# A bidirectional encoder trunk on one core: short convolution's projections leave PSUM by ScalarE, a cross product becomes one operation, and the filling products come in another order

## The chip, the cores and the metric

The kernel runs on one core of one Trainium2 chip. The metric is the device time of one launch in microseconds (us). PE is the matrix engine (TensorE), DVE is VectorE, ACT is ScalarE, POOL is GpSimd, and SP is the engine whose queue issues most of the DMA transfers. Each engine takes its own instructions strictly in order.

## The reference, cut to what matters

One layer over 1024 tokens of width 1024, all in float32. A normalised input `h` is multiplied by one wide matrix. Its columns feed four token mixers and 32 gates; the mixers' outputs are gated and added, and cross attention and a feed-forward network follow. The change touches the mixers named S5, RG-LRU and short convolution.

```
hr, hi = a2r*b1r - a2i*b1i + b2r, a2r*b1i + a2i*b1r + b2i          # S5: complex h_t = a h_{t-1} + b_t
r  = sigmoid(xc @ wa + ba);  i = sigmoid(xc @ wx + bx)             # RG-LRU, per direction, xc = conv4(xr)
la = -8 * r * softplus(-lam)
h  = scan(exp(la), sqrt(-expm1(2 * la)) * (i * xc))                # h_t = exp(la)_t h_{t-1} + b_t
y  = b_gate * conv3(c_gate * xin)                                  # short convolution
decay = exp(gam_c - gam_d) for c >= d                              # gated DeltaNet, in the phase behind
```

## The kernel before, in words

Channels lie on the 128 partitions and the 1024 tokens along the free axis. A projection of 128 output columns is 48 matmuls of 128x512 (three products of split float32 halves, `mm3`), called from L171. PE's order is written by hand: two matmuls are one *step*, so a projection is 24 steps. Projections that nothing else orders stand in a queue of generators (`Fill`), and `fill(n)` pulls n steps from it between the matmuls of the S5 mixer. So while DVE works through S5's sequential recurrence, PE works off the queue.

The queue holds six gates (a gate is one projection and a tanh on ACT, `tho`, stored to DRAM as `thd`) and four *pairs*. `pair(j)` interleaves `lru(j)` with `short_conv(j)`. PE's order in a pair is: LX 24 steps, LG 24, la0 2, SC 24, li0 2, SX 24, la1 2, SB 24, li1 2. LX, LG, SC, SX and SB are projections. la0, li0, la1 and li1 are small products with `lw` (L403 before, L407 after). Between them ACT and DVE compute the two directions of the RG-LRU, in the tiles `la`, `li`, `lt`, `hf`, `gl`, and the short convolution, in `sa` and `sb`.

Projections and small products share the PSUM pool `pp`, which has **two** tiles of 128x1024. PE can't start a product until the one two before it has been read out of PSUM. The order of the other engines is fixed when the kernel is built; each weight block of 128x512 is also split into two halves there, `wh` by ACT and `wl` by POOL.

The stretch of the program around the change runs in this order: `s5_in` (eight parts, 52 steps of fill), `Scalars.run` (70 steps; it needs the small weights `wba` and a table `cst`, loaded into boxes of S-phase's ring), `s5_scan` (17 turns of 16 steps), 12 steps, `s5_out` (eight parts of 12), 48 steps, `s5_glu` (four parts of 6, which read S5's output back from DRAM: `zbuf`, `cm`, `H`), then the rest of the queue, 82 steps. Then comes the DeltaNet phase (`GPhase`). Its tiles take the room of the S phase, so its first loads (`w<-in_cst`) wait for the last store of that phase (`yd<-hf`). They feed casts on DVE (`gcr`), products on POOL (`Bn`, `G`, `dgl`), and these the first matmuls of `decays` (L990 and L992 before, L993 and L995 after), ahead of which PE has one projection, Q/K/V block 4.

All tiles in the ring have one buffer per name. Line numbers in the kernel after the change are 3 to 5 higher.

Of the kernel before, what the change touches and what calls it, by code (L numbers as in the profile page):

```python
# [11 lines left out]
F32 = mybir.dt.float32  # L12
F32R = mybir.dt.float32r
AF = mybir.ActivationFunctionType
# [4 lines left out]
P = 128  # L19
# [5 lines left out]
ADD, SUB, MUL, MAX, MIN = ALU.add, ALU.subtract, ALU.mult, ALU.max, ALU.min  # L25
# [292 lines left out]
class SPhase:  # L318
# [25 lines left out]
    def short_conv(self, j):  # L344
        K, nc = self.K, self.nc
        pc = yield from self.project(SC + j)
        c = self.big("sa")
        nc.scalar.activation(c, pc, AF.Copy)
        yield False
        px = yield from self.project(SX + j)  # L350
        K.tt(c, px, c, MUL)
        cv = self.big("sb")
        K.conv(cv, c, K.v("sconv", 3 * j, 3), 1)
        yield False
        pb = yield from self.project(SB + j)
        K.tt(cv, pb, cv, MUL)
        nc.sync.dma_start(K.yd[3, j], cv)
        yield False

# [25 lines left out]
    def lru(self, j):  # L385
        K, nc = self.K, self.nc
        lw = self.ring.tile([P, 2, 2, P], F32, name="lw")
        nc.sync.dma_start(lw, K.a["lw"][j])
        xc = self.big("xc")
        K.conv(xc, (yield from self.project(LX + j)), K.v("lconv", 4 * j, 4), 2, K.v("lconvb", j))  # L390
        yield False
        pg = yield from self.project(LG + j)
        gl = self.big("gl")
        nc.scalar.activation(gl, pg, AF.Gelu_apprx_tanh)
        yield False
        hs = []
        for d in range(2):
            i = 4 * d + j
            tg = []
            for k, b in ((0, self.hba), (1, self.hbx)):  # L400
                ps = K.pp.tile([P, S], F32, name="pp")
                for o in (0, 512):
                    nc.tensor.matmul(ps[:, o:o + 512], lw[:, k, d], xc[:, o:o + 512], start=True, stop=True)  # L403
                    if o == 0:
                        yield True
                t = self.big(("la", "li")[k])
                nc.scalar.activation(t, ps, AF.Tanh, bias=b[:, i:i + 1], scale=0.5)  # L407
                tg.append(t)
                yield False
            thr, thi = tg  # L410
            a, t2 = thr, self.big("lt")
            nc.scalar.activation(t2, thr, AF.Tanh, bias=self.c4[:, i:i + 1], scale=self.c4[:, i:i + 1])
            nc.scalar.activation(a, thr, AF.Exp, bias=self.c2n[:, i:i + 1], scale=self.c2n[:, i:i + 1])
            K.stt(a, a, 1.0, t2, ADD, MUL)
            K.ts(a, a, -1.0, 1.0, MUL, ADD)
            nc.scalar.activation(t2, t2, AF.Sqrt)
            K.stt(t2, a, 1.0, t2, ADD, MUL)
            K.stt(thi, thi, 1.0, xc, ADD, MUL)
            K.tt(thi, thi, t2, MUL)
            h = self.big("hf") if d == 0 else t2  # L420
            r = (lambda x: x) if d == 0 else (lambda x: x[:, ::-1])
            nc.vector.tensor_tensor_scan(r(h), r(a), r(thi), 0.0, MUL, ADD)
            hs.append(h)
        K.tt(hs[0], hs[0], hs[1], ADD)
        K.stt(hs[0], hs[0], 0.5, gl, MUL, MUL)
        nc.sync.dma_start(K.yd[2, j], hs[0])
# [127 lines left out]
    def s5_in(self):  # L554

        K, nc, fill = self.K, self.nc, self.fill
        s5 = self.s5
        late = []
        for o in range(8):
            t = self.tmps()  # L560
            self.cmul(self.apb, s5[:, 0], s5[:, 1], o, t)
            wb = [self.ring.tile([P, 4, 8, 16], F32, name=f"wb{d}") for d in range(2)]
            lo, hi = slice(0, 64), slice(64, P)
            for i, op in ((0, SUB), (1, ADD)):
                K.tt(t[2 * i], t[2 * i], t[2 * i + 1], op)
                r = (lo, hi)[i]
                nc.scalar.activation(wb[0][r], t[2 * i][lo], AF.Copy)
                nc.vector.tensor_copy(wb[1][r], t[2 * i][hi])
            u = self.load_u(o)
            wt = []  # L570
            for i in range(2):
                ps = K.sm.tile([P, 4, P], F32, name="sm")
                for g in range(4):
                    nc.tensor.transpose(ps[:, g], t[2 * i][:, g], K.ident)
                wt.append(self.ring.tile([P, 4, P], F32, name=f"wt{i}"))
                nc.scalar.activation(wt[i], ps, AF.Copy)
            L = self.big("L").rearrange("p (g n) -> p g n", g=4)[0:16, :, 0:240]
            for q in range(2):
                pl = K.sm.tile([P, 512], F32, name="sm")[0:16, 0:480].rearrange("p (g n) -> p g n", g=2)
                for g2 in range(2):  # L580
                    g = 2 * q + g2
                    c0 = 64 * o + 16 * g
                    cf, cb = [x[:, c0:c0 + 16] for x in self.cd]
                    nc.tensor.matmul(pl[:, g2, 0:P], cf, wb[0][:, g], start=True, stop=False)
                    nc.tensor.matmul(pl[:, g2, P - 16:P], cb, wb[1][:, g, 0], start=False, stop=True)
                    nc.tensor.matmul(pl[:, g2, P:240], cb, wb[1][:, g, 1:8], start=True, stop=True)
                nc.scalar.activation(L[:, 2 * q:2 * q + 2], pl, AF.Copy)
            tT = self.ring.tile([P, 4, P], F32, name="tT", bufs=2)
            for k in range(8):
                nc.sync.dma_start(tT[16 * k:16 * k + 16], L[:, :, (7 - k) * 16:(7 - k) * 16 + P])  # L590
            for i in range(2):
                pv = K.sm.tile([P, 4, P], F32, name="sm")
                for g in range(4):
                    nc.tensor.matmul(pv[:, g], wt[i][:, g], u[:, g], start=True, stop=True)
                c0 = 32 * i + 4 * o
                h = self.H[:, :, c0:c0 + 4].rearrange("p c g -> p g c")
                nc.scalar.activation(h[0:64], pv[0:64], AF.Copy)
                nc.vector.tensor_copy(h[64:P, :, ::-1], pv[64:P])
            late.append((o, tT))
            fill(5)  # L600
            if o:
                self.s5_turn(*late.pop(0))
        fill(12)
        self.s5_turn(*late.pop(0))
# [19 lines left out]
    def s5_scan(self):  # L624

        K = self.K
        H = self.H.rearrange("p (a k) n -> p a k n", k=8)
        t0, t1 = [self.big(f"cm{i}").rearrange("p (a n) -> p a n", a=16) for i in range(2)]

        def turn(out, a, x):  # L630
            n = x.shape[1]
            ri = lambda y: y.rearrange("p n (r g) -> p n r g", r=2)
            b = lambda y: y.unsqueeze(1).to_broadcast([P, n, 64])
            for r in range(2):
                y = slice(32 * r, 32 * r + 32), slice(32 - 32 * r, 64 - 32 * r)
                K.tt(t1[:, :n, y[0]], b(a[1])[:, :, y[0]], x[:, :, y[1]], MUL)
            K.tt(out[:, :n], b(a[0]), x, MUL)
            K.tt(out[:, :n], out[:, :n], t1[:, :n], ADD)

        for k in range(1, 8):  # L640
            turn(t0, self.a8, H[:, :, k - 1])
            K.tt(H[:, :, k], H[:, :, k], t0, ADD)
            yield
        for a in range(1, 16):
            turn(t0, self.a64, H[:, a - 1:a, 7])
            K.tt(H[:, a:a + 1, 7], H[:, a:a + 1, 7], t0[:, 0:1], ADD)
            if a % 5 == 0:
                yield
        for k in range(7):
            turn(t0, self.a8, t0[:, 0:15] if k else H[:, 0:15, 7])  # L650
            K.tt(H[:, 1:16, k], H[:, 1:16, k], t0[:, 0:15], ADD)
            yield
# [1241 lines left out]
def tile_trunk(ctx, tc, a, out):  # L1894
    ctx.enter_context(tc.manual_schedule(engines={mybir.EngineType.PE}))
    K = _K(ctx, tc, a)
    nc = tc.nc
    big = ctx.enter_context(tc.tile_pool(name="big", bufs=1))
    h = big.tile([P, 2, KD, S], F32R, name="big")
    hh, hl = h[:, 0], h[:, 1]  # L1900
# [13 lines left out]
    fill = Fill()  # L1914
    with tc.tile_pool(name="tho", bufs=1, side="right") as tp, ExitStack() as gs:
        gates = [gate_tile(K, tp, i, hh, hl) for i in range(32)]
        sc = Scalars(K, gs)
        with ExitStack() as c:
            s = SPhase(K, c, hh, hl, fill)
            fill.add(*gates[:5])  # L1920
            for j in range(4):
                fill.add(s.pair(j))
            fill.add(*gates[5:6])
            s.s5_prep()
            s.s5_c()
            s.lru_prep()
# [2 lines left out]
            s.s5_in()  # L1929
            waits = [12, 12, 46, 0]  # L1930
            scan = s.s5_scan()
            for go in sc.run(hh, hl, s.parts("xc", "gl", "cm0")):
                if not go:
                    fill(waits.pop(0))
            K.lo = "pool"
# [11 lines left out]
        with ExitStack() as c:  # L1947
            g = GPhase(K, c, hh, hl, fill, sc)
# [49 lines left out]
```

## Time and profile before

| | |
|---|---|
| time, median of 3 runs | 2467.16 us (2465.7 to 2467.51) |
| time of the profiled execution | 2468.41 us |
| span of the profiled execution | 2466.6 us |
| mean granted clock of PE | 0.981 |

The span is what the trace covers; the time of the same execution is 1.8 us longer, and it is 1.25 us above the median. The granted clock is the share of its full 2.4 GHz that PE was given; 0.50 is its lower level, 1.2 GHz.

### The profile page before, as it was taken

Reading aid. Unit: us, or ns where it says so; the run is one execution under the profiler, and the core shown is the slowest. Engines: PE = TensorE matmul, PEld = TensorE weight load, DVE = VectorE, ACT = ScalarE, POOL = GpSimd, SP = SyncE. Lnnn points to the kernel's source line nnn. Section 1 sums busy time; section 2 is a strip of 40 time slices with the busy share of each in tenths; the row PEclk is TensorE's granted clock in tenths of the full one; section 3 lists DMA queues with packets and bytes.
Section 4 is the critical chain, followed back from the end, with each engine's and each line's share of the span. In section 5 each row is a group of like instructions: output and inputs, shape, how many; then the busy total and the mean of one; then the engine's idle time right before and its main releaser. Section 6 shows DMA issues by size and latency. Waiting matters only on the chain. (4 is left out here: it accounts for less than half of the span.)

```text
span 2466.6 us, 31800 instructions
## 1 busy us (share of the span) xinstructions
PE 2367.3 (96%) x11495; PEld 1924.4 (78%) x11495; DVE 1501.5 (61%) x2991; ACT 932.7 (38%) x1461; POOL 886.9 (36%) x636
## 2 busy tenths in 40 slices
PE   7999989899999999999999999999999999999998
PEld 6777767778878788787778888888788888877886
DVE  5883998845937758569336543274777666661421
ACT  6372434534324123232222133255444444443431
POOL 6422224435324233232122222204344444445443
PEclk8999999999999999999999999999999999999998
DMA  7443112432211211111165443106322222245541
GB/s 261 115 109 101 36 63 77 116 133 75 69 45 50 65 49 55 60 56 65 48 238 176 149 152 123 45 1 200 99 77 78 85 95 77 86 146 180 186 163 55
DMA packets 136205, 250.44 MB, mean 102 GB/s; under 512 B 15344, under 2 KB 42992, under 8 KB 135920
## 3 DMA queue, kind: packets, MB, share of 16 engines
q1 hardware_dynamic: 136048, 248.41, 31.3%
q8 instruction: 91, 1.49, 0.3%
q14 instruction: 66, 0.54, 0.1%
HBM read 188.58 MB, written 57.67 MB: 100 GB/s over the span
## 5 line engine op out<-in xcount | busy, mean ns | idle before, releaser
L142 POOL TENSOR_TENSOR wl<-wr,wh 128x512 fp32r<-128x512 f32 x507 | 694.0, 1376 | 1333.6 <-ACT wh L140 1146.2
L171 PE MATMUL pp<-big,wh 128*128 128x512 f32 x2560 | 728.7, 402 | 16.2 <-DVE sa L192 12.5
L140 ACT ACTIVATE wh<-wr 128x512 fp32r<-128x512 f32 (+1 forms) x526 | 322.2, 621 | 983.9 <-PE pp L171 517.7
L171 PEld LDWEIGHTS pp<-big,wh 128*128 128x128 f32 x2560 | 474.3, 191 | 118.5 <-DVE sa L192 14.8
L171 PE MATMUL pp<-big,wl 128*128 128x512 f32 x1280 | 406.4, 399 | 0.0
L1479 PE MATMUL sm<-big,wh 128*128 128x512 f32 x1152 | 363.1, 396 | 4.6 <-DVE big L142 2.5
L1479 PE MATMUL sm<-bigq,wh 128*128 128x512 f32 x1040 | 327.2, 396 | 4.2 <-ACT sm L1691 3.0
L171 PEld LDWEIGHTS pp<-big,wl 128*128 128x128 f32 x1280 | 237.7, 190 | 48.1
L1479 PEld LDWEIGHTS sm<-big,wh 128*128 128x128 f32 x1152 | 217.7, 189 | 55.9 <-DVE big L142 3.8
L1479 PEld LDWEIGHTS sm<-bigq,wh 128*128 128x128 f32 x1040 | 195.9, 189 | 51.7 <-ACT sm L1691 3.4
L1479 PE MATMUL sm<-big,wl 128*128 128x512 f32 x576 | 226.3, 393 | 0.0
L1479 PE MATMUL sm<-bigq,wl 128*128 128x512 f32 x520 | 203.9, 392 | 0.0
L171 PE MATMUL pp<-yhl,wh 128*128 128x512 f32 x512 | 137.3, 390 | 2.4 <-DVE acc L189 1.3
L1479 PEld LDWEIGHTS sm<-big,wl 128*128 128x128 f32 x576 | 109.1, 189 | 24.5
L1479 PEld LDWEIGHTS sm<-bigq,wl 128*128 128x128 f32 x520 | 98.0, 188 | 22.0
L171 PEld LDWEIGHTS pp<-yhl,wh 128*128 128x128 f32 x512 | 95.9, 188 | 23.5 <-DVE acc L189 1.7
L189 DVE SCALAR_TENSOR_TENSOR pp<-ut,vec,pp 128x1023 f32<-128x1023 f32 x88 | 113.0, 1284 | 1.6
L192 DVE TENSOR_TENSOR bigq<-bigq,sm 128x512 f32<-128x512 f32 x16 | 10.9, 684 | 125.1 <-PE sm L1479 125.1
L1758 ACT ACTIVATE pp<-ut,vec 128x1024 f32<-128x1024 f32 x44 | 53.2, 1210 | 69.2 <-DVE ut L192 69.2
L192 DVE TENSOR_TENSOR y<-y,t 128x8 f32<-128x8 f32 (+30 forms) x248 | 79.3, 359 | 0.0
L171 PE MATMUL pp<-yhl,wl 128*128 128x512 f32 x256 | 78.8, 389 | 0.0
L192 DVE TENSOR_TENSOR t<-rb,x 128x8 f32<-128x8 f32 (+30 forms) x248 | 78.4, 355 | 0.0
(417 smaller groups left out, 3337.8 us busy)
## 6 DMA issues: line engine op xcount, KB each, us to landing
wr<-in_wi SPq DMA_DIRECT2D x144, 256.0 KB, 2.7
wr<-in_wup SPq DMA_DIRECT2D x88, 256.0 KB, 4.2
wr<-in_wdn SPq DMA_DIRECT2D x80, 256.0 KB, 4.2
thd<-tho SPq DMA_DIRECT2D x32, 512.0 KB, 2.9
thi<-thd SPq DMA_DIRECT2D x32, 512.0 KB, 4.1
gd<-sg SPq DMA_DIRECT2D x22, 512.0 KB, 2.9
gr<-gd SPq DMA_DIRECT2D x44, 256.0 KB, 4.1
wr<-in_wkv SPq DMA_DIRECT2D x32, 256.0 KB, 3.7
```

Of the source, the lines that this page charges most:

```text
L140: self.nc.scalar.activation(hi, src, AF.Copy)
L142: e.tensor_tensor(lo, src, hi.bitcast(F32), SUB)
L171: self.nc.tensor.matmul(ps[:, o:o + step], w[:, i], r[:, k, o:o + step], start=first, stop=last)
L189: self.nc.vector.scalar_tensor_tensor(out, in0, s, in1, op0, op1)
L192: (eng or self.nc.vector).tensor_tensor(out, a, b, op)
L1479: self.K.nc.tensor.matmul(ps, a[:, i], b, start=start and i == 0 and j == 0, stop=last and stop is not False, skip_group_check=stop is Non ...
L1758: K.nc.scalar.activation(c[b], t[b], AF.Identity, bias=K.v("fconvb", n), scale=K.v("fconv", 3 * n + 1))
```

## The change

Five edits. Short convolution's SX and SB products are copied out of PSUM by ACT into a new box `sc`, and DVE multiplies from there; `s5_in` takes the same box for its `wb`. In the RG-LRU the step `1 - a` goes from a DVE operation to an ACT one. In the S5 recurrence two products on halves of 32 columns become one product on a view with the halves swapped. The queue's order becomes gates 0 to 2, pair 0, gates 3 to 5, pairs 1 to 3 (before: gates 0 to 4, pairs 0 to 3, gate 5). And `Scalars.run` takes other boxes.

```
         px = yield from self.project(SX + j)
-        K.tt(c, px, c, MUL)
+        x = self.big("sc")
+        nc.scalar.activation(x, px, AF.Copy)
+        K.tt(c, x, c, MUL)
         cv = self.big("sb")
         K.conv(cv, c, K.v("sconv", 3 * j, 3), 1)
         yield False
         pb = yield from self.project(SB + j)
-        K.tt(cv, pb, cv, MUL)
+        x = self.big("sc")
+        nc.scalar.activation(x, pb, AF.Copy)
+        K.tt(cv, x, cv, MUL)
...
             K.stt(a, a, 1.0, t2, ADD, MUL)
-            K.ts(a, a, -1.0, 1.0, MUL, ADD)
+            nc.scalar.activation(a, a, AF.Identity, bias=1.0, scale=-1.0)
             nc.scalar.activation(t2, t2, AF.Sqrt)
...
-            wb = [self.ring.tile([P, 4, 8, 16], F32, name=f"wb{d}") for d in range(2)]
+            wb = self.big("sc").rearrange("p (d g t j) -> p d g t j", d=2, g=4, t=8)
+            wb = [wb[:, d] for d in range(2)]
...
-            for r in range(2):
-                y = slice(32 * r, 32 * r + 32), slice(32 - 32 * r, 64 - 32 * r)
-                K.tt(t1[:, :n, y[0]], b(a[1])[:, :, y[0]], x[:, :, y[1]], MUL)
+            K.tt(ri(t1[:, :n]), ri(b(a[1])), ri(x)[:, :, ::-1], MUL)
...
-            fill.add(*gates[:5])
-            for j in range(4):
+            fill.add(*gates[:3], s.pair(0), *gates[3:6])
+            for j in range(1, 4):
                 fill.add(s.pair(j))
-            fill.add(*gates[5:6])
...
-            for go in sc.run(hh, hl, s.parts("xc", "gl", "cm0")):
+            for go in sc.run(hh, hl, s.parts("L", "cm1", "cm0")):
```

ACT's order at the second direction (la1) of pair 0, before. `sb<-sa` starts short convolution's second convolution, `lt<-lt` is the square root:

```order
L203 ACTIVATE sb<-sa,vec 128x1024 [waits DVE_49]
L407 ACTIVATE la<-pp,hba 128x1024 [waits PE_49]
L412 ACTIVATE lt<-la,c_1092 128x1024 [waits Activation_49]
L413 ACTIVATE la<-la,c2n 128x1024 [waits Activation_49]
L140 ACTIVATE wh<-wr 128x512 [waits DMAHW0_49,PE_49,Pool_49]
L416 ACT_TABLE_LOAD
L416 ACTIVATE lt<-lt 128x1024 [waits DVE_49]
L140 ACTIVATE wh<-wr 128x512 [waits DMAHW1_49,PE_49,Pool_49]
```

The same place in the kernel after:

```order
L352 ACTIVATE sc<-pp 128x1024 [waits PE_49]
L411 ACTIVATE la<-pp,hba 128x1024 [waits DVE_49,PE_49]
L416 ACTIVATE lt<-la,c_1092 128x1024 [waits Activation_49]
L203 ACTIVATE sb<-sa,vec 128x1024 [waits DVE_49]
L417 ACTIVATE la<-la,c2n 128x1024 [waits Activation_49]
L140 ACTIVATE wh<-wr 128x512 [waits DMAHW2_49,PE_49,Pool_49]
L419 ACTIVATE la<-la 128x1024 [waits DVE_49]
L420 ACT_TABLE_LOAD
L420 ACTIVATE lt<-lt 128x1024
L140 ACTIVATE wh<-wr 128x512 [waits DMAHW3_49,PE_49,Pool_49]
L359 ACTIVATE sc<-pp 128x1024 [waits PE_49]
```

The copy of SX is the first of these rows, the copy of SB the last; between them stand three operations that wait for DVE, one of them the new `la<-la`.

SP's order where `Scalars` loads its small weights, before, in the middle of `s5_in`:

```order
L533 DMA ubuf<-sb 16x8x128 [waits DMAHW4_49]
L152 DMA wr<-in_wi 128x512 [waits DMAHW5_49,DVE_49]
L757 DMA xc<-in_cst 128x256 [waits DMAHW6_49,DVE_49,Pool_49]
L759 DMA xc<-in_wba 128x128 [waits DMAHW7_49]
L152 DMA wr<-in_wi 128x512 [waits DMAHW0_49,DVE_49]
```

And after, at the end of `s5_in`, where the box is `L`:

```order
L595 DMA tT<-L 16x4x128 [waits DMAHW1_49]
L618 DMA tbuf<-tt 128x512 [waits DMAHW2_49,Activation_49]
L1199 DMA thd<-tho 128x1024 [waits DMAHW3_49,Activation_49]
L760 DMA L<-in_cst 128x256 [waits DMAHW5_49,DMAHW6_49,DMAHW4_49,DMAHW7_49,DMAHW1_49,DMAHW0_49]
L762 DMA L<-in_wba 128x128
L152 DMA wr<-in_wi 128x512 [waits DVE_49]
```

The two loads have moved behind the last eight `tT<-L` transfers, which read the box that they write.

ACT's order from the last square root of the S phase to the first `E` of the next phase, before (`li<-pp` reads li1 of pair 3; two `wh` stand for a projection):

```order
L416 ACTIVATE lt<-lt 128x1024 [waits DVE_49]
L140 ACTIVATE wh<-wr 128x512 [waits DMAHW4_49,PE_49,Pool_49]
L407 ACT_TABLE_LOAD
L407 ACTIVATE li<-pp,hbx 128x1024 [waits PE_49]
L140 ACTIVATE wh<-wr 128x512 [waits DMAHW5_49,PE_49,Pool_49]
L140 ACTIVATE wh<-wr 128x512 [waits DMAHW6_49,PE_49,Pool_49]
L1195 ACTIVATE tho<-pp 128x1024 [waits PE_49]
L140 ACTIVATE wh<-wr 128x512 [waits DMAHW0_49,PE_49,Pool_49]
L140 ACTIVATE wh<-wr 128x512 [waits DMAHW2_49,PE_49,Pool_49]
L203 ACTIVATE w_4853<-pp,vec 128x1024 [waits DMAHW4_49,DMAHW3_49,DMAHW7_49,DVE_49,PE_49]
L995 ACTIVATE E<-sm,g_ngam 128x128 [waits PE_49]
```

And after:

```order
L420 ACTIVATE lt<-lt 128x1024
L140 ACTIVATE wh<-wr 128x512 [waits DMAHW7_49,PE_49,Pool_49]
L359 ACTIVATE sc<-pp 128x1024 [waits PE_49]
L411 ACT_TABLE_LOAD
L411 ACTIVATE li<-pp,hbx 128x1024 [waits PE_49]
L140 ACTIVATE wh<-wr 128x512 [waits DMAHW0_49,PE_49,Pool_49]
L140 ACTIVATE wh<-wr 128x512 [waits DMAHW1_49,PE_49,Pool_49]
L203 ACTIVATE w_4832<-pp,vec 128x1024 [waits DMAHW3_49,DMAHW1_49,DMAHW6_49,DVE_49,DMAHW7_49,PE_49,Activation_49]
L998 ACTIVATE E<-sm,g_ngam 128x128 [waits PE_49]
```

The projection of gate 5, with its `tho`, no longer stands between li1 and the first `E`; it runs during the scan. PE's order from `decays` on is the same in both kernels.

## Rows read from the trace of the kernel before

**Rows 1.** The page, busy time of each engine.
```profile
PE 2367.3 (96%) x11495; PEld 1924.4 (78%) x11495; DVE 1501.5 (61%) x2991; ACT 932.7 (38%) x1461; POOL 886.9 (36%) x636
```

**Rows 2.** Windows (start:end, length, busy PE, PEld, DVE, ACT, POOL; clock): scan, `s5_out`, rest.
```profile
244.00:390.00 146.00, 133.53 (x532) 102.94 (x531) 138.15 (x186) 59.89 (x63) 39.20 (x22) 0.95 0.16 55
390.00:478.00 88.00, 76.93 (x404) 64.14 (x403) 76.48 (x94) 46.94 (x50) 36.99 (x37) 0.96 0.33 96
478.00:600.00 122.00, 118.81 (x495) 93.41 (x494) 60.70 (x48) 52.92 (x71) 56.95 (x32) 0.99 0.36 118
```

**Rows 3.** PE's waits from 190 to 600 us: total, times, longest.
```profile
PE pp L171 <- DVE sa L192: 12.5, 3, 6.2
PE sm L675 <- DVE L L671: 4.6, 2, 3.9
...
PE pp L171 <- DVE sb L192: 1.8, 1, 1.8
```

**Rows 4.** Windows behind the longest waits, columns as in group 2.
```profile
296.00:304.00 8.00, 7.19 (x20) 5.69 (x21) 7.62 (x22) 4.63 (x4) 0.00 (x0) 0.58 0.01 3
...
368.00:376.00 8.00, 7.12 (x20) 5.68 (x21) 8.00 (x9) 3.52 (x3) 0.00 (x0) 0.60 0.00 0
...
412.00:420.00 8.00, 7.21 (x31) 6.51 (x31) 4.84 (x6) 1.99 (x2) 2.42 (x5) 0.58 0.42 115
...
486.00:492.00 6.00, 6.00 (x20) 4.74 (x20) 3.18 (x2) 2.75 (x4) 4.60 (x2) 0.72 0.45 120
```

**Rows 5.** DVE's groups by line and shape, 244 to 600 us: busy, mean ns.
```profile
L192 DVE TENSOR_TENSOR cm<-a,H 128x512 f32<-128x512 f32 x12 | 12.0, 1039 | 0.1
...
L189 DVE SCALAR_TENSOR_TENSOR xc<-pp,vec,xc 128x1023 f32<-128x1023 f32 x8 | 10.2, 1278 | 0.1
...
L192 DVE TENSOR_TENSOR cm<-cm,cm 128x1024 f32<-128x1024 f32 x7 | 9.5, 1355 | 0.1
...
L199 DVE TENSOR_SCALAR la<-la 128x1024 f32<-128x1024 f32 x8 | 6.6, 826 | 0.1
...
L192 DVE TENSOR_TENSOR sa<-pp,sa 128x1024 f32<-128x1024 f32 x4 | 4.9, 1218 | 5.0 <-PE pp L171 5.0
```

**Rows 6.** ACT's groups by line and shape, 190 to 600 us.
```profile
L416 ACT ACT_TABLE_LOAD x8 | 10.3, 1283 | 0.1
...
L203 ACT ACTIVATE sb<-sa,vec 128x1024 f32<-128x1024 f32 x4 | 4.6, 1152 | 9.6 <-DVE sa L192 9.6
...
L348 ACT ACTIVATE sa<-pp 128x1024 f32<-128x1024 f32 x4 | 4.0, 1005 | 0.0
```

**Rows 7.** Timeline where the scan begins: PE's first filling product, DVE's first operation.
```profile
243.06 0.70 PE L171 MATMUL pp<-big,wl 128*128 128x512 f32 x2
...
244.22 1.23 DVE L192 TENSOR_TENSOR cm<-a,H 128x1024 f32<-128x1024 f32 x1
```

**Rows 8.** Timeline and DMA issues at `Scalars`: SP's last `tT<-L`, PE's wait.
```profile
191.17 5.07 SPq L590 DMA_DIRECT2D tT<-L  x8
...
198.08 0.63 PE L610 MATMUL sm<-ident,tT 128*128 128x128 f32 x4 [2.59 <-issue]
198.47 1.17 PE L171 MATMUL pp<-big,wbah 128*16 128x512 f32 x4
```

**Rows 9.** Timeline where the phases meet, PE, DVE and POOL.
```profile
570.92 1.88 PE L403 MATMUL pp<-xc,lw 128*128 128x512 f32 x4
...
594.44 0.39 PE L990 MATMUL sm<-gcr 128*128 128x512 f32 x1
...
590.39 0.97 DVE L828 CAST gcr<-w 128x128 fp32r<-128x128 f32 x1 [0.88 <-DMA w<-in_cst]
...
593.09 1.90 POOL L192 TENSOR_TENSOR dgl<-gcr,g_gl 128x1024 fp32r<-128x1024 f32 x1
```

**Rows 10.** Timeline behind the last `s5_out`: SP's stores, ACT's next splits of `H`.
```profile
477.46 3.60 SPq L682 DMA_DIRECT2D zbuf<-tt  x8
...
486.19 1.04 ACT L140 ACTIVATE H<-cm 128x1024 fp32r<-128x1024 f32 x1
```

## The prediction, on record before the changed kernel ran

> **What bounds the kernel now.** The busy times come first: PE works 96% of the span, no other engine over 61% [rows 1]. Nothing PE computes is added or removed, so the time can only change where PE waits, or where its clock is lower. The next view is windows by stage, for the stretch that the edits touch. Idle time is length less PE's busy time: 12.5 us in the scan, 11.1 in `s5_out`, 3.2 behind it, 26.7 in all [rows 2].
>
> The view of waits names the owners: 12.5 us in three waits for DVE's `sa` multiplication, the longest 6.2 (two of them end at the scan's windows of group 4, one stands late in `s5_out`); 4.6 for DVE's copies `L`, nearly all in one wait of 3.9; one of 1.8 for `sb` [rows 3]. Behind four of these the granted clock was lower: 0.58, 0.60 and 0.58 over 8 us, 0.72 over 6 us [rows 4]. What was not granted, times PE's busy time there, is 0.42 x 7.19 = 3.0, 0.40 x 7.12 = 2.8, 0.42 x 7.21 = 3.0 and 0.28 x 6.00 = 1.7 us. So **the waits of 3.9 to 6.2 us each cost about 2.9 us on top of themselves**, and the one of 1.8 has cost 1.7; for a new wait of 4 us or more I add 2.9, for a shorter one less. What is to be priced is waits plus clock: 26.7 + 10.5 = 37 us before.
>
> **The change part by part.**
>
> *1. The copies.* A DVE multiplication that reads PSUM takes 1.22 us [rows 5], as long as its neighbours in SBUF, so reading from a copy makes DVE no faster. What changes is who frees the PSUM tile. Before, SX's tile waits for DVE to reach its multiplication, and DVE is 138.15 of 146 us busy in the scan [rows 2]. After, it waits for an ACT copy, 1.0 us [rows 6]. In ACT's order only weight splits stand between li0's tanh and SX's copy, and the 2 steps of la1 (1.5 to 1.9 us [rows 9]) cover it. So the three `sa` waits should vanish: -12.5, with the clock of two of them -5.8: **-18.3**. Bounds: 0, if the copy is as late as the multiplication was, and -18.3.
>
> The Trainium skill, in VectorE: DVE Perf Modes, Rules for kernel authors, says of elementwise work on a matmul's output to accept the slower read of PSUM, or to copy to SBUF first if many operations will read it. Here one reads it, so by that rule the copies are work for nothing and this term would be 0; the wait for DVE's place in line, which the rows show, is outside the rule.
>
> *2. The S5 product.* Two products on halves cost 2 x 1.04 us where POOL's work collides with them, against 1.36 for a whole-width addition [rows 5]. The merged one lies between 1.2 and 2.1. DVE is no longer waited for by the copies, so this is worth 0 by itself; it enters in 4.
>
> *3. `Scalars`' loads.* They move behind the eight transfers out of `L`, whose issue ends at 191.17 + 5.07 = 196.24 [rows 8]. Each must land, then the loads, then ACT's split. If the two landings take 2 us each, PE gets `wba` at about 200.5, not 198.47: 2.0 us (0 to 4). This lengthens a wait of 2.59, so the clock may fall too; I count 1.0. **+3.0**.
>
> *4. Pair 0's end.* Pair 0 now runs early in the scan. With the scan's first operation PE begins SC. To gate 3, the next product, are SC, li0, SX, la1, SB and li1. A projection is 10.9 us: 594.44 - 570.92 = 23.5 holds li1 (about 1.6) and two of them [rows 9]. That is 3 x 10.9 + 3 x 1.6 = 37.5 us after PE's first step, 1.2 ahead of DVE's first [rows 7]. Gate 3 needs the tile of SB, so the copy of SB, last in ACT's rows shown with the change. Ahead of it stands the new `la<-la`, which waits for a DVE operation that DVE's order puts behind 4 turns and a quarter of S5. Up to there DVE has five plain products (1.22 like `sa`), four merged ones (1.6, the middle of 2) and eight additions (1.36): 5 x 1.22 + 4 x 1.6 + 8 x 1.36 = 23.4 [rows 5]. Seven operations of the pair at 1.25 and a recurrence, counted as two of them, make 11.2 more. DVE's start is itself some 2 us later, since ACT now has la0's tanh and a table load (1.15 + 1.28 [rows 6]) ahead of the value that the scan waits for. So `la<-la` starts at about 1.2 + 2 + 34.6 = 37.8; then 1.15 for itself, a table load of 1.28, square root and copy 1.0 each and a split of half their width, about 0.6, end at 42.8 [rows 6]. PE waits 42.8 - 37.5 = 5.3; with the merged product at its ends, 3.8 to 7.2. Plain operations take 1.22 where POOL is quiet, as it is while PE waits, so I take **4.5 + 2.9 of clock = +7.4**. If the copy were served at once, it would be 0.
>
> *5. Pair 1's end.* The same rows stand there, `sc<-SB` behind `la<-la` and the square root, and DVE has S5's output preparation ahead. By the reckoning of 4 that is 0 to 7 us; the preparation is made of shorter operations than S5's turns, so I take the lower middle, 3.0, and 2.0 of clock: **+5.0**.
>
> *6. `s5_out`.* DVE's three operations of pair 1's second direction and three of a convolution, about 9 us, stood ahead of the `L` copies that PE waited 3.9 us for. Most of them now come earlier or later: -3.9 - 3.0 of clock + 2.0 that comes back with the later convolution, **-5.0** (bounds -7 and 0).
>
> *7. Pair 2's copy of SX* falls behind `s5_out`. In ACT's new order it stands behind the third split of `H`, whose load SP issues behind eight stores. Before, those stores begin at 477.46, the split that follows their load starts at 486.19 and takes 1.04 [rows 10], so the copy ends near 488. PE wants the tile 10 steps and la1 after `s5_out`'s end (some 0.9 us ahead of the stores): 476.6 + 4.5 + 1.9 = 483. So 4.3 to 5 + 2.9, against `sb`'s 1.8 + 1.7 before: **+3.7** (-3.5 to +5).
>
> *8. `s5_glu`.* LX of pair 3 now ends inside `s5_glu`. Its convolution, three DVE operations of 1.28 [rows 5] behind an ACT one of 1.15 [rows 6], 5.0 us, is what the next part's product waits for, and 4 steps of 0.46 stand between: 3.0, and 1.5 of clock: **+4.5** (0 to 7).
>
> *9. Where the phases meet.* Before, li1 begins at 570.92 and `decays` at 594.44 without a wait, behind gate 5 and block 4 [rows 9]. The chain beside them: tanh, recurrence, store `yd<-hf`, load, cast until 590.39 + 0.97 = 591.36, POOL's products until 593.09 + 1.90 = 594.99. The first `decays` need the cast, the last the products. The cover was just enough: gate 5 hid it. Now gate 5 is done in the scan, and PE arrives after li1 and block 4 alone, 1.6 + 10.9 = 12.5 us behind li1's start. The cast ends 20.4 us behind it, the products 24.1. PE waits 7.9, then works 1.4, then waits some 2.3. I take 9.5 (8 to 11) and 2.9 of clock: **+12.4**. POOL and SP lose gate 5's split and store, which may bring the chain 1 us forward; ACT's copy of SB puts it back by half of one.
>
> The 1 - a step itself (DVE 0.83 [rows 5], ACT about 1.15 [rows 6]) is in 4 and 5. Q/K/V and all behind has the same order; no wait is moved there.
>
> **Sum.** -18.3 + 3.0 + 7.4 + 5.0 - 5.0 + 3.7 + 4.5 + 12.4 = +12.7 us. The profiled execution took 2468.41, its span 2466.6 and 1.8 around it, so the one after would take 2481.1; that execution was 1.25 above the median, so against the median it is **2480 us**.
>
> **The rivals.** A difference under 0.2%, 4.9 us, can't be told from no change.
> - *The ACT queue is no bottleneck* (faster). Terms 4, 5, 7 and 8 rest on ACT being held by DVE's results at the moment of a copy; ACT is busy only 60 of 146 us in the scan [rows 2], and if DVE runs 6 us ahead of my count, all four copies are served at once. Then -18.3 + 3.0 - 5.0 - 3.5 + 12.4 = -11.4: 2456. It is faster once the four come to less than 9 us, where I count 20.6. Against it: each place has a row in ACT's order that must wait, and DVE is 95% busy.
> - *Half of it* (no change). Two of the four waits, or the end's chain shortened and covered elsewhere: -5 to +5, 2462 to 2472. The terms of 12.4 and -18.3 then nearly cancel.
> - *The copies free nothing* (much slower): SX's copy is itself held in ACT's line by a waiting operation, as in 4, and the scan's waits stay. That is the sum without its first term: +31, 2498. Against it: only splits stand ahead of SX's copy in pair 0. The rule of term 1 ends here as well.
>
> **How the numbers follow.** Forecast, all or most of the four waits come: 0.53. ACT no bottleneck: 0.17. Half: 0.23. Copies free nothing: 0.07. So slower 0.53 + 0.07 = 0.60, same 0.23, faster 0.17. The bounds of the terms of the forecast alone give about 2470 to 2492. The range reaches down into the faster case and leaves out its lower part and the copies' case: 2460 to 2492.
>
> **What would show it.** Right: in the view of waits, no `sa` from the scan on; a wait of 8 us or more for `gcr`, `Bn` or `dgl` ahead of `decays`; waits of 3 to 7 us at the first matmul of gate 3 and of pair 2's LX, released by ACT's `sc`, with the clock at 0.5 to 0.6 behind them; 4 to 5 us ahead of `wbah`. What would make it wrong: `decays` without a wait would take away 12.4 us and turn the sign; ACT's copies starting within a microsecond of PE's end would take away 20.

## The result and the profile after

The changed kernel takes 2492.48 us (median of 4 runs, 2490.15 to 2495.45), the one before 2467.34 beside it: a ratio of 1.0101, 95% interval [1.0083, 1.0118]. It is slower, as forecast, but by 25 us where 13 were forecast, and half a microsecond above the range.

The page of the kernel after, busy time of each engine; the span is 2493.3 us:

```profile
PE 2376.9 (95%) x11495; PEld 1930.8 (77%) x11495; DVE 1501.1 (60%) x2953; ACT 947.2 (38%) x1477; POOL 883.6 (35%) x637
```

PE's busy time is 9.6 us longer for the same matmuls; the lower clock, worked out below, comes to 9.2. The view of waits of the kernel after, PE, 100 to 650 us (total, times, longest):

```profile
PE pp L171 <- ACT sc L359: 12.6, 2, 7.5
PE sm L993 <- DVE gcr L831: 6.6, 1, 6.6
PE sm L615 <- DMA tT<-L: 4.7, 3, 2.6
PE pp L171 <- ACT sc L352: 4.5, 1, 4.5
PE pp L171 <- DVE xc L189: 4.1, 1, 4.1
PE pp L407 <- issue: 4.1, 1, 4.1
PE sm L678 <- DVE L L674: 3.3, 2, 3.0
PE pp L171 <- ACT wbah L140: 2.6, 1, 2.6
PE sm L679 <- DVE L L674: 2.5, 3, 1.0
...
PE sm L995 <- POOL dgl L192: 0.8, 1, 0.8
PE sm L995 <- POOL Bn L192: 0.3, 1, 0.3
```

The three waits for `sa` [rows 3] are gone. In their place stand ACT's copies: `sc` of L359 (SB, 7.5 us ahead of gate 3 and 5.2 ahead of pair 2's LX) and of L352 (SX of pair 2, 4.5). The waits for `gcr`, `xc` and `wbah` are new, and so is one that was not forecast: 4.1 us at pair 1's la0 (L407, which the view puts down to issue).

Windows of the kernel after by stage (columns as in [rows 2]): scan to the second part of `s5_out`, the rest of `s5_out`, and up to `decays`.

```profile
253.00:420.00 167.00, 149.49 (x629) 118.23 (x628) 156.23 (x170) 70.79 (x78) 50.12 (x31) 0.95 0.18 61
420.00:480.00 60.00, 54.95 (x292) 46.31 (x291) 51.68 (x66) 33.18 (x36) 23.48 (x27) 0.94 0.42 121
480.00:624.00 144.00, 126.28 (x497) 97.31 (x496) 66.52 (x51) 66.97 (x83) 56.33 (x33) 0.93 0.30 96
```

The first of these is the one to look at. PE is idle for 17.5 of 167 us. In the kernel before, the same piece of work reads:

```profile
244.00:416.00 172.00, 153.52 (x631) 120.03 (x630) 162.40 (x209) 68.47 (x72) 52.36 (x31) 0.95 0.18 58
```

18.5 of 172 us. All the waits for DVE's `sa` went, and PE waits nearly as long as before. The larger loss is behind it: 17.7 us idle from 480 us on, against 3.2 [rows 2]. Windows of the kernel after behind its longest waits show the clock:

```profile
200.00:208.00 8.00, 6.54 (x18) 2.32 (x19) 0.29 (x1) 0.31 (x1) 0.00 (x0) 0.57 0.50 155
292.00:300.00 8.00, 4.52 (x12) 3.61 (x13) 7.99 (x7) 5.82 (x6) 1.79 (x1) 0.57 0.19 66
356.00:364.00 8.00, 8.00 (x25) 5.57 (x26) 7.86 (x8) 4.89 (x4) 0.00 (x0) 0.79 0.01 2
400.00:412.00 12.00, 9.37 (x42) 8.05 (x43) 9.10 (x7) 5.94 (x7) 2.29 (x4) 0.72 0.33 111
456.00:464.00 8.00, 7.13 (x29) 6.52 (x30) 7.58 (x11) 5.46 (x7) 3.67 (x5) 0.57 0.26 62
490.00:496.00 6.00, 5.35 (x17) 4.32 (x18) 4.15 (x2) 5.28 (x6) 2.41 (x2) 0.72 0.59 143
528.00:532.00 4.00, 3.97 (x11) 3.22 (x12) 0.00 (x0) 0.00 (x0) 0.00 (x0) 0.59 0.20 76
612.00:624.00 12.00, 9.36 (x21) 6.43 (x22) 9.23 (x6) 6.29 (x18) 10.87 (x7) 0.52 0.10 29
```

Share not granted times PE's busy time, as in the prediction: 2.8, 1.9, 1.7, 2.6, 3.1, 1.5, 1.6 and 4.5, in all 19.7 us, against 10.5 before [rows 4]: the 9.2 us more.

The timeline where the phases meet, kernel after: li1 on PE, DVE's last operation of the pair and first cast, POOL's last product, PE's `decays`.

```profile
594.11 1.88 PE L407 MATMUL pp<-xc,lw 128*128 128x512 f32 x4
...
613.53 0.77 PE L993 MATMUL sm<-gcr 128*128 128x512 f32 x1 [6.64 <-DVE gcr L831]
...
618.92 0.79 PE L995 MATMUL sm<-dgl,gcr 128*128 128x512 f32 x1 [0.78 <-POOL dgl L192]
...
605.25 1.22 DVE L189 SCALAR_TENSOR_TENSOR hf<-hf,gl 128x1024 f32<-128x1024 f32 x1
...
611.11 0.23 DVE L831 CAST gcr<-w 128x128 fp32r<-128x128 f32 x1 [1.13 <-DMA w<-in_cst]
...
616.97 1.90 POOL L192 TENSOR_TENSOR dgl<-gcr,g_gl 128x1024 fp32r<-128x1024 f32 x1
```

From li1's start to the first `decays` are 19.4 us, with one projection of PE's work in them; before they were 23.5 with two [rows 9]. DVE's chain ends 12.4 us behind li1's start (605.25 + 1.22), and then only the store, the load and the casts are waited for.

### The profile page after: what moved, and what is told of

It reads as the page before. It is cut to its first block, busy times and chain, and to the rows that moved or that the text cites. A ratio compares the mean times of both kernels' runs of the same rounds, so it can differ in the third digit from the quotient of the medians.

```text
span 2493.3 us, 31776 instructions
## 1 busy us (share of the span) xinstructions
PE 2376.9 (95%) x11495; PEld 1930.8 (77%) x11495; DVE 1501.1 (60%) x2953; ACT 947.2 (38%) x1477; POOL 883.6 (35%) x637
## 5 line engine op out<-in xcount | busy, mean ns | idle before, releaser
L171 PE MATMUL pp<-big,wh 128*128 128x512 f32 x2560 | 733.3, 405 | 18.5 <-ACT sc L359 12.6
L192 DVE TENSOR_TENSOR bigq<-bigq,sm 128x512 f32<-128x512 f32 x16 | 10.9, 683 | 125.2 <-PE sm L1482 125.2
L192 DVE TENSOR_TENSOR y<-y,t 128x8 f32<-128x8 f32 (+30 forms) x248 | 79.1, 358 | 0.0
L192 DVE TENSOR_TENSOR t<-rb,x 128x8 f32<-128x8 f32 (+30 forms) x248 | 78.2, 354 | 0.0
```

The lines of the kernel that those rows point to most:

```text
L171: self.nc.tensor.matmul(ps[:, o:o + step], w[:, i], r[:, k, o:o + step], start=first, stop=last)
L192: (eng or self.nc.vector).tensor_tensor(out, a, b, op)
```

## The experiments

Each run has its own runs of the kernel before beside it; the ratios are to those. The first theory (A) was that the queue's order makes the loss and the copies are a gain; its rival (B) that the work moved to ACT makes it. Edits are to the kernel after, if nothing else is said.

**Order of the queue apart from the rest.** Two runs split the change in its halves. The first has the old order and the old boxes of `Scalars`, with copies, step on ACT and merged product:

```
-            fill.add(*gates[:3], s.pair(0), *gates[3:6])
-            for j in range(1, 4):
+            fill.add(*gates[:5])
+            for j in range(4):
                 fill.add(s.pair(j))
+            fill.add(*gates[5:6])
...
-            for go in sc.run(hh, hl, s.parts("L", "cm1", "cm0")):
+            for go in sc.run(hh, hl, s.parts("xc", "gl", "cm0")):
```

> The changed kernel with the old queue order and the old boxes of Scalars; copies, step on ACT and merged product stay. Theory A (the order of the queue makes the loss: pair 0 falls into the wide turns of the scan, nothing covers the phases' meeting; the copies are a gain): the sa waits stay away, gate 3, pair 1's la0 and the meeting no longer wait, so before's 2467 less 12.5 of waits and 5.8 of clock, 2447 to 2456. Theory B (ACT's copies and the step are at fault, wherever they stand): waits for sc of 10 us or more in all stay, 2475 to 2492.

Measured: 2471.28, ratio 1.0016 [1.0003, 1.0029], about 4 us slower than before. Neither theory: the order is what costs most, but the copies are no gain. Its waits, PE, 190 to 640 us:

```profile
PE pp L171 <- ACT sc L359: 13.7, 3, 6.9
PE pp L171 <- ACT sa L348: 3.1, 1, 3.1
PE pp L171 <- ACT cm L702: 3.1, 1, 3.1
...
PE pp L407 <- ACT gl L398: 2.6, 1, 2.6
```

No `sa L192`, and 13.7 us for `sc`, where `sa` had taken 12.5 [rows 3]. The second run is the kernel before with the new order and boxes alone (the same edit the other way round).

> The kernel before with the new queue order and the new boxes of Scalars alone. Theory A: the meeting of the phases waits 7 to 8 us with 4 of clock, Scalars' load 5, and without the copies SX's tile of pair 0 is freed only by DVE's multiplication, about 7 us later than the copy was, in the place of gate 3's wait: 2490 to 2510, as slow as the whole change or slower. Theory B: no waits for ACT's copies, so clearly faster than the whole change, 2470 to 2482.

Measured: 2491.55, ratio 1.0104 [1.0081, 1.0127]: the whole loss, without any copy. Theory A's part on the order holds.

**Which part of the order.** Gate 5 back at the end:

```
-            fill.add(*gates[:3], s.pair(0), *gates[3:6])
+            fill.add(*gates[:3], s.pair(0), *gates[3:5])
             for j in range(1, 4):
                 fill.add(s.pair(j))
+            fill.add(*gates[5:6])
```

> The changed kernel with gate 5 put back at the queue's end; gates 3 and 4 stay behind pair 0. Theory A: decays no longer waits, so 7.75 of wait and 4.4 of clock go, 2480 if nothing else moves; pairs 1 to 3 come 24 steps earlier, so waits in s5_out and s5_glu may go or come, 2474 to 2487. Rival (the chain there is late whatever PE does before): 2490 to 2494.

Measured: 2478.58, ratio 1.0047 [1.0029, 1.0065]; from 1.0101 that is 13 us. `decays` begins without a wait. The rival is out. Next, the first box of `Scalars` moved:

```
-            for go in sc.run(hh, hl, s.parts("L", "cm1", "cm0")):
+            for go in sc.run(hh, hl, s.parts("hf", "cm1", "cm0")):
```

> The changed kernel with Scalars' first box moved from L to hf, which nothing uses at that time, so that its loads need not wait for the transfers out of L. Theory A: the wait of 2.6 us ahead of wbah and its 2.7 of clock go, -5: 2485 to 2489, all later waits as they were. Rival (the load was late for another reason, or what PE wins there it loses at gate 3, since DVE sets that time): 2490 to 2493, with gate 3's wait grown from 7.5 to 10 or more.

Measured: 2488.05, ratio 1.0094 [1.0072, 1.0115]. The wait ahead of `wbah` is gone and gate 3's is 7.5 us as it was, but alone the gain is not clear of the intervals. The profiled execution is the slowest of its four (2493.79, the others 2488): a single wait of 2.4 us is left at `Scalars`, and in that execution the clock fell behind it all the same, to 0.57 from 198 to 202 us:

```profile
198.00:202.00 4.00, 3.23 (x11) 1.70 (x12) 0.00 (x0) 0.60 (x1) 0.21 (x2) 0.57 1.01 292
```

Both together:

> The changed kernel with gate 5 last and Scalars' first box in hf, both. If the two losses add up: 2492.5 - 13.9 - 4.4 = 2474 (2470 to 2478). If what PE wins at Scalars is lost at gate 3, whose time DVE sets: 2478, the same as with gate 5 last alone.

Measured: 2471.32, ratio 1.0014 [1.0004, 1.0025]. That is 8 us below gate 5 last alone, so the box counts, and within the intervals the losses add up. It is also the time of the old order in full (1.0016): that pair 0 stands ahead of gates 3 and 4 costs nothing that can be told.

**Who holds the tiles.** Old order and boxes, SX copied, SB multiplied out of PSUM by DVE, the step on DVE:

```
-        x = self.big("sc")
-        nc.scalar.activation(x, pb, AF.Copy)
-        K.tt(cv, x, cv, MUL)
+        K.tt(cv, pb, cv, MUL)
...
-            nc.scalar.activation(a, a, AF.Identity, bias=1.0, scale=-1.0)
+            K.ts(a, a, -1.0, 1.0, MUL, ADD)
```

> Old queue order and old boxes of Scalars; SX is copied by ACT, but SB is multiplied out of PSUM by DVE and the step 1 - a is on DVE again; the merged product stays. Theory C (the chain of a pair through DVE and ACT is what PE waits for; a copy moves the wait from SX's tile to SB's, whoever frees that): no wait for sa, but waits for sb of 10 to 14 us in all in their place, 2462 to 2472. Theory D (the wait behind SB's copy is ACT's own line: the step, the table load and the square root ahead of it): with SB left to DVE no such wait, 2447 to 2456.

Measured: 2466.94, ratio 0.9993 [0.9983, 1.0002]. The time is theory C's: no wait for DVE's `sa`, and 8.7 us for `sb`, a little under what it said, and 4.7 for `li` come instead (PE, 190 to 640 us):

```profile
PE pp L171 <- DVE sb L192: 8.7, 2, 5.4
...
PE pp L171 <- ACT li L409: 4.7, 1, 4.7
```

The step alone put back to DVE, in the kernel after (the second half of the edit):

> The changed kernel with the step 1 - a on DVE as before. Theory D: the step is a good part of what SB's copy waits behind, its 1.06 us goes from each of the eight chains and the DVE operation of 0.7 comes two rows later, waits for sc fall from 12.6 to about 10: 2486 to 2490. Theory C: DVE is the line that is waited for and gets the work back: 2490 to 2494.

Measured: 2492.73, ratio 1.0098 [1.0083, 1.0113]: no change that can be told, so theory D's gain did not come. Its waits for L359 fall from 12.6 to 4.5 us, and L352's rise from 4.5 to 8.7:

```profile
PE pp L171 <- ACT sc L352: 8.7, 2, 4.6
...
PE pp L171 <- ACT sc L359: 4.5, 1, 4.5
```

Then a version made to get both tiles free ahead of the chain, in the old order and with the step on DVE: SX, SB and only then la1 and li1.

```
         x = self.big("sc")
         nc.scalar.activation(x, px, AF.Copy)
+        yield False
+        pb = yield from self.project(SB + j)
+        g = self.big("sb")
+        nc.scalar.activation(g, pb, AF.Copy)
         K.tt(c, x, c, MUL)
-        cv = self.big("sb")
+        cv = self.big("sc")
         K.conv(cv, c, K.v("sconv", 3 * j, 3), 1)
...
-        gens = [self.lru(j), self.short_conv(j)]
+        a, b = self.lru(j), self.short_conv(j)
+        for g in (a, a, a, b, a, b, b, a, a):
```

> Old queue order and boxes, step on DVE, merged product, both copies by ACT; but SB's projection now stands ahead of the second direction's small products, so that its copy is ahead of that chain in ACT's order too (C by ACT to sa, X to sc, B to sb, the convolution into sc). Theory C: neither tile waits for the chain any more, so before's three sa waits go and nothing comes in their place: 12.5 + 5.8 us less, 2447 to 2456. Rival (the chain is waited for elsewhere, at li1 or the next pair's LX): 2460 to 2470 with a wait for la or li of 4 us or more.

Measured: 2470.22, ratio 1.0010 [1.0000, 1.0019]. Of the waits for `sa`, `sb` and `sc` only two of about 1 us are left, for copies by ACT, and nothing is won. The two longest waits, and the timeline of DVE ahead of the longest:

```profile
PE sm L675 <- DVE L L671: 12.4, 1, 12.4
PE pp L404 <- issue: 6.3, 1, 6.3
```

```profile
399.82 2.29 DVE L423 TENSOR_TENSOR_SCAN lt<-la,li 128x1024 f32<-128x1024 f32 x1
402.14 1.22 DVE L192 TENSOR_TENSOR hf<-hf,lt 128x1024 f32<-128x1024 f32 x1
...
409.26 3.09 DVE L671 COPY L<-H 64x508 f32<-64x508 f32 x2
```

PE comes to the second `s5_out` 12 us ahead of DVE, which goes through its line without a gap. So theory C was too narrow: PE waits here not for the chain of a pair but for all that stands in DVE's line up to `L`.

**DVE's amount of work.** The kernel before without one addition in each turn of S5's recurrence:

```
             K.tt(out[:, :n], b(a[0]), x, MUL)
-            K.tt(out[:, :n], out[:, :n], t1[:, :n], ADD)
```

> The kernel before without the addition of the two products in each turn of S5's recurrence: 14 wide and 15 narrow DVE operations, 23 us of DVE in the scan, are left out, PE's work stays. Theory E (from the scan's start to the second part of s5_out DVE's line is the bound, and PE waits there for DVE at whichever tile comes first): the two sa waits of the scan and the waits for wt and L behind it go, 16.6 us of waits and 8.6 of clock, at most what DVE saves: 2442 to 2450. Rival (PSUM's two tiles and the order in which they are freed set these waits, not DVE's amount of work): two or more of the waits stay at 3 us or more, 2457 to 2467.

Measured: 2451.49, ratio 0.9934 [0.9915, 0.9952], 16 us less: between the two, 1.5 us above theory E's range and 5.5 below the rival's. From the scan's start to the second `s5_out` the same 631 matmuls take 157 us instead of 172, and PE's idle time falls from 18.5 to 7.6 us, with the same PSUM tiles, freed by the same operations:

```profile
244.00:401.00 157.00, 149.44 (x631) 117.09 (x630) 141.39 (x183) 68.76 (x73) 54.94 (x31) 0.98 0.19 63
```

It isn't all of the 25 us of waits and clock: waits for `sa` of 4.4 us stay, 3.5 at one place. The trace shows what stands ahead there. The build fixes DVE's order, and without the additions it puts the products of twelve narrow turns of S5 ahead of that `sa`, where the kernel before has one; `sa` starts at 295.11 us, against 295.54. The merged product alone, on the kernel before:

```
-            for r in range(2):
-                y = slice(32 * r, 32 * r + 32), slice(32 - 32 * r, 64 - 32 * r)
-                K.tt(t1[:, :n, y[0]], b(a[1])[:, :, y[0]], x[:, :, y[1]], MUL)
+            K.tt(ri(t1[:, :n]), ri(b(a[1])), ri(x)[:, :, ::-1], MUL)
```

> The kernel before with the merged product alone. Theory E: DVE has 0 to 5 us less in its line, so PE's waits in the scan shrink by as much: 2462 to 2467. If the merged form with the halves swapped costs DVE more than the two it replaces: 2468 to 2475.

Measured: 2463.39, ratio 0.9980 [0.9971, 0.9990], 5 us less, inside theory E's range. Of the five edits it is the only one shown to gain, and this kernel is faster than the one before and the changed one.

**More work for PE in that stretch.** The kernel before with gates 6 and 7 drawn forward, and then the same on the kernel with SX's copy alone:

```
-            fill.add(*gates[:5])
-            for j in range(4):
+            fill.add(*gates[:5], gates[6], s.pair(0), gates[7])
+            for j in range(1, 4):
                 fill.add(s.pair(j))
-            fill.add(*gates[5:6])
+            fill.add(gates[5])
...
-                fill(16)
-            fill(12)
+                fill(18)
+            fill(26)
...
-        fill.add(*gates[6:])
+        fill.add(*gates[8:])
```

> The kernel before with 48 more steps of PE work in the DVE-bound stretch: gates 6 and 7 are drawn forward from the DeltaNet phase's queue, one ahead of pair 0 and one behind it; the scan's turns take 18 steps instead of 16, and 26 instead of 12 follow it. Theory E: PE does that work, 21.8 us, where it waits now, and the phase behind is shorter by as much if it can spare two gates: 16 to 22 us less, 2445 to 2452. Rival (the DeltaNet phase needs its gates as cover, or the waits stand at other tiles): 2460 to 2470.

Measured: 2472.16, ratio 1.0019 [1.0010, 1.0029]: above both ranges, and against theory E. Its trace shows two reasons. First, PE did only a part of the added 21.8 us where it had waited. From the scan's start to the second `s5_out` DVE is busy for 168 us, PE still idles for 12.9 (before 18.5), 8.2 of them for `sa`, and the stretch is some 15 us longer than before:

```profile
245.00:432.60 187.60, 174.73 (x723) 136.96 (x722) 168.49 (x209) 72.99 (x78) 52.77 (x35) 0.95 0.19 63
```

Second, in the phase behind, two waits stand that the kernel before doesn't have (PE, 600 to 2460 us):

```profile
PE sm L1186 <- DVE QK L192: 6.1, 1, 6.1
PE pp L171 <- ACT yhl L1213: 4.6, 1, 4.6
```

`decays` begins 12 us later than before, and from there to the end the run takes 1866.1 us against 1872.2: 6 us less, though 21.8 us of PE's work are gone from that phase. So it can't spare its gates either.

> As the run with two more gates, on the kernel that has the merged product and ACT's copy of SX alone. Theory E: no better than two more gates alone by more than what the merged product saves, 2440 to 2452. Theory D (a copy by ACT takes PE off DVE's line): 8 us or more below the run without it.

Measured: 2465.91, ratio 0.9993 [0.9984, 1.0002]: the same as SX's copy without them, and 6 us below the run without copy and merged product. That lies between what theory E allows for the merged product (5) and theory D's 8 or more, and the time is above theory E's range for the two reasons named (both waits of the phase behind stand in its trace too, 6.1 and 4.6): this pair of runs decides nothing between D and E.

## Why the prediction was wrong

The prediction was right on the sign and on most places, and wrong on the size. Terms by stage, from windows (idle time plus clock, after less before):

| stage | terms | forecast | measured |
|---|---|---|---|
| `Scalars` | 3 | +3.0 | +5.4 |
| scan to the second `s5_out` | 1, 4, 5, 6 | -10.9 | -3.6 |
| rest of `s5_out` | in 6 | 0 | +3.1 |
| behind `s5_out`, to `decays` | 7, 8, 9 | +20.6 | +20.4 |
| sum | | +12.7 | +25.3 |

Measured: `Scalars`, a new wait of 2.6 and 2.8 of clock. Scan: idle 17.5 against 18.5, clock 1.9 + 1.7 + 2.6 = 6.2 against 3.0 + 2.8 + 3.0 = 8.8. Rest of `s5_out`: idle about 5 in both, clock 3.1. Behind: 17.7 + 1.5 + 1.6 + 4.5 against 3.2 + 1.7. The medians differ by 25 us, the two profiled executions by 27.

- **The step that failed is the adding up of the scan's terms.** Term 1 booked 18.3 us as won because the `sa` waits would vanish, and terms 4 and 5 booked two new waits as if these were the whole price, 7.4 + 5.0 = 12.4. The `sa` waits did vanish. But the waits that came in their place cost 23.0: 7.5 + 1.9 at gate 3, 5.2 + 2.6 at pair 2's LX, and 4.1 + 1.7 at a place that had no term. What PE didn't wait for at one tile it waited for at the next: five kernels that free the tiles in five ways have PE idle for 16 to 20 us from the scan's start to the second `s5_out` (windows: before 18.5, after 17.5, old order with all copies 16.0, SX's copy alone 16.9, SB ahead of la1 20.3). DVE's line is what it waits for there: leaving out DVE work gave 7.6. The row was in view, DVE 138 of 146 us busy [rows 2]; it served to explain the waits, not to doubt that they could be booked as won. That DVE's work alone sets the stretch's length is not shown, and the run with two more gates speaks against it: with PE's work added the stretch grew by some 15 us, and PE still idled for 12.9.
- **A wait was missed**, 4.1 us and 1.7 of clock at pair 1's la0. Its convolution stands in DVE's line among the wide turns of the scan; DVE finished it at 355.88 (354.61 + 1.27) and PE began at 355.98. It is DVE's line once more.
- **Term 2** was taken as 0, and the merged product alone gains 5 us. Busy time of the products of a turn, kernel before and merged, 244 to 600 us:

```profile
L192 DVE TENSOR_TENSOR cm<-a,H 128x512 f32<-128x512 f32 x12 | 12.0, 1039 | 0.1
...
L192 DVE TENSOR_TENSOR cm<-a,cm 128x480 f32<-128x480 f32 x12 | 9.5, 829 | 0.0
...
L192 DVE TENSOR_TENSOR cm<-a,H 128x1024 f32<-128x1024 f32 x7 | 8.5, 1216 | 0.0
L192 DVE TENSOR_TENSOR cm<-a,cm 128x960 f32<-128x960 f32 x6 | 6.9, 1148 | 0.1
```

```profile
L192 DVE TENSOR_TENSOR cm<-a,H 128x1024 f32<-128x1024 f32 x13 | 19.6, 1546 | 0.1
...
L192 DVE TENSOR_TENSOR cm<-a,cm 128x960 f32<-128x960 f32 x12 | 14.9, 1243 | 0.1
```

  Halves and plain ones took 12.0 + 9.5 + 8.5 + 6.9 = 36.9 us, merged and plain ones 34.5; the narrow turns save about as much again. It would be near to say that this is the gain, but the traces don't show it so: from the scan's start to the second `s5_out` DVE is busy for 162.4 us in both kernels, since other operations of its line took longer (the seven additions `H<-H,cm` of 128x960 11.9 us instead of 8.9), and PE idles for 18.5 and 18.4. The difference stands behind: from there to `decays` PE idles for 8.3 us before and 5.9 with the merged product, at a mean clock of 0.99 and 1.00. How the lighter product brings that about stays open.
- **Term 3** had the place and the wait (2.0, measured 2.6, as a second wait behind the first); the clock fell by its full price (2.8), where 1.0 was counted.
- **Terms 7, 8 and 9 were right**, 20.6 against 20.4, with their places. Term 9 is borne out by the run with gate 5 last, 13 us. That it fits so closely is in part luck: the wait is smaller than forecast (7.7 against 9.5) and the loss of clock larger (4.5 against 2.9).
- **The rule weighed at term 1** (the Trainium skill, VectorE: DVE Perf Modes, Rules for kernel authors) would have had that term at 0. The sum would then have been 2498, nearer to the 2492 measured, but the scan's part farther off (+7.4 where -3.6 was measured), and for another reason: the copies did free SX's tile early, and PE then waited elsewhere.
- **One bound of a rival is wrong in itself.** Without the four waits of terms 4, 5, 7 and 8 the sum is -7.9, so for a gain of 4.9 us or more they would have to come to less than 3 us, not 9.

By edits the 25 us are, from the ratios: the merged product -5, copies and step about +9 over it (1.0016 against 0.9980), the queue's order and `Scalars`' boxes +21 (1.0101 against 1.0016), of which gate 5's place is 13 and the box 8. That is one way of taking the edits in turn; put first, on the kernel before, order and boxes cost 26 by themselves (1.0104), and the other three then come to nothing.

Where the 9 us stand, the traces of the old order with all copies and of the merged product alone show. With the copies PE is through the second `s5_out` 4.5 us sooner after the scan's start. But from the last part of `s5_out` to `decays` it takes 125.5 us (470.9 to 596.4) against 115.8 (471.8 to 587.6), with waits of 3.7 for `sc` and 3.1 for `cm` among them and the clock at 0.96 against 1.00:

```profile
471.00:596.00 125.00, 117.57 (x479) 92.16 (x478) 56.05 (x44) 53.84 (x59) 47.06 (x28) 0.96 0.34 111
```

```profile
472.00:588.00 116.00, 113.78 (x481) 89.53 (x480) 56.88 (x46) 48.37 (x55) 49.25 (x28) 1.00 0.36 119
```

What stays open: how the 9 us divide between SX's copy, SB's copy and the step (SX's copy alone, 0.9993 against 0.9980, is 3, and those intervals overlap), how the merged product gains its 5, and what part the two tiles of `pp` have in the waits: no run has a third one.

## What to carry to other kernels

Before a wait is booked as won, ask what the waiting engine meets next. Where another engine is 95% busy over the stretch, an earlier release can simply move the wait to the next tile; here taking work off that engine counted for more (16 us) than freeing tiles sooner (none to be told), and giving the waiting engine more to do filled only about a third of its gaps. Compare the idle time of the whole stretch, not the wait that vanished. Work that fills gaps has a second duty at the end of its queue: whatever stands last covers the chain into the next phase, so price the cover before moving it. A load that is given another buffer waits for that buffer's last reader; look up where that reader stands in the queue.

## What the runs showed of the hardware

A short wait doesn't always have the same price. At `Scalars` ten traces have a single wait of PE of 2.4 to 2.7 us. In seven of them the granted clock stayed at 1.00 behind it, as in the kernel before [rows 8]; in three it fell to its lower level, 1.2 GHz, for a few us (a mean of 0.57 over 4 us in the run with the box `hf` alone, behind 2.45 us of wait). The length doesn't tell them apart: 2.72 us without a fall, 2.41 us with one. In the four traces with a second wait, of 2.6 us, behind one group of transposes, the clock fell every time; in the kernel after it is 0.57 from 200 to 208 us. The window of that stage in the kernel before:

```profile
190.00:244.00 54.00, 51.41 (x237) 37.70 (x236) 16.65 (x61) 10.79 (x17) 14.18 (x6) 1.00 0.30 97
```

Reading an operand with its halves swapped cost DVE nothing. In the run with the merged product alone, 13 of the 14 products of 128x960 in the last seven turns of the scan took 1.15 or 1.16 us, swapped and plain ones alike, and one took 2.26. Two halves of 128x480 that ran undisturbed took 0.65 each. So the means shown under term 2 (1243 for 128x960, 829 for the halves) are mixtures: most operations have the short time, and a few, beside POOL's splits, about a microsecond more. Term 2 took such means for the price of each operation.

```profile
342.52 1.15 DVE L192 TENSOR_TENSOR cm<-a,cm 128x960 f32<-128x960 f32 x1
...
344.72 2.26 DVE L192 TENSOR_TENSOR cm<-a,cm 128x960 f32<-128x960 f32 x1
```
